# Inputs, ranks and slots of the first experts earlier, down biases in the last sums, row tiles at multiples of 128 bytes, in a two-block kernel with 32 routed experts

## The chip, the cores and the metric

One core of one Trainium2 chip runs the whole program. The metric is device time in microseconds (us). The engines are PE (TensorE; PEld its weight loads), DVE (VectorE), ACT (ScalarE), POOL (GpSimd) and SP (SyncE, which here only issues transfers).

## What is computed

Two blocks in sequence on 512 tokens of width 1024, all fp32. The first has a gated linear recurrence, retention and spatial gating, twice; the second is attention with a short convolution and then a mixture of experts. The change lies between the router of that mixture and the end:

```
h2 = modulate(x, g_norm2, sh2, sc2)               # 512 x 1024
logits = h2 @ w_router + b_router                 # 32 experts
top_logit, top_idx = top_k(logits, 4); gate = softmax(top_logit)
for each expert e, for the rows of h2 routed to it:
    gu = h2[rows] @ w_gate_up[e] + b_gate_up[e]   # 1024 x 2048
    y  = clamped_swiglu(gu) @ w_down[e] + b_down[e]
    moe[rows] += gate * y
x = x + gt2 * moe
out = rmsnorm(x, g_final)
```

Each expert brings 12 MB of fp32 weights, 384 MB for all.

## The kernel before

**Dense part and router, to about 1285 us.** Matmuls run as three passes: `split` (L288 to L291) makes a rounded high part on ACT (L289) and the remainder on DVE (L290), and PE multiplies high by high, high by low and low by high. `router` computes logits on the raw rows `hr`, takes the four best (`mask`), the position of each token within its expert (`pos`, by matmuls with triangular ones, `cum`), the counts (`cnt`), and the gates as high and low parts in `vals`. It also makes the modulated rows, in four pieces of 512 x 256 called `raw` and `tv`, scaled by 1/rms (`nat`), and stores them to DRAM as `h_rows`.

**Experts, from about 1295 us.** `moe` goes through `ORDER`: 0, 1, 16, 2, 17, 3 and so on. The 32 experts are ranked by load (`ranks`: matmuls `kc`, `rk`, `perm`); the upper 16 ranks are "wide" (up to 128 rows, three-pass weights through `wsplit`), the lower 16 "narrow" (64 rows, plain fp32 weights). Experts 0 and 1 are wide and are taken by their own number, before ranking. Weights come as 384 tiles of 1 MB: `wload` issues them on SP's queue into eight buffers in rotation. The fourth buffer first holds the staging of the gate-up bias, and the eighth lies on memory of `tv`.

For a pair of experts, `slots` finds which token sits in which row: it picks the pair's positions and gates by rank (`pick`), builds one-hot rows (`oh`), multiplies (`slot`, `slotT`), and makes indices; then POOL gathers their rows of `h_rows` into `xgn` (narrow) or `xg` (wide). `inputs` transposes them on PE (`xT<-xgn`, `xT<-xg`, L1518). Experts 0 and 1 need no DRAM: `first_slots` makes one-hots `hots` from `pos`, and `first_inputs` gathers by matmul (`xT<-hots,hr`, L1428), with evictions (`x<-xT`) by ACT (L1434) and DVE (L1432) in turn and a split. `gate_up`, `narrow_gate_up`, `down` and `narrow_down` compute; POOL adds the weighted results `ye` into the DRAM rows `x_rows` by index. `residual` (L1310) multiplies the down biases by the gates (`xt<-gb,gT`), adds them to `hr` and stores it as the first content of `x_rows`. At the end `finish` adds the last two experts from SBUF (`fx`) to the rows read back, and normalises.

**What sets the order.** In the router and the first expert the tile scheduler orders each engine, by priority (`high_priority(AHEAD)`) and by "not before" marks (`issue_after`, `behind`). From the second expert on `in_order` keeps the order in which the program is written. `work()` in `moe` is a list of steps; `fill` takes one step after each quarter of an expert's gate-up or down part, so that `slots` and `inputs` of later experts are spread over the current one. In the kernel before, the slots of 0 and 1 and then of 16 are made during expert 0 behind the second `first_inputs` and the ranks; those of 2 during expert 1:

```
slots[max(before(p - 3 - 2 * (narrow and p > 6)), 1 - narrow)].append((r, narrow))
```

Of the kernel before, what the change touches and what calls it, by code (L numbers as in the profile page):

```python
# [203 lines left out]
class Kern:  # L204
# [134 lines left out]
    def consts(self):  # L339
# [13 lines left out]
        self.mod = c.tile([128, 2, 48], F32, name="mod")  # L353

# [676 lines left out]
    def router(self):  # L1031
# [92 lines left out]
        nc.vector.tensor_add(pos, pos, pc[:, :128].rearrange("p (b e) -> p b e", b=4))  # L1124

# [5 lines left out]
        with tc.high_priority(AHEAD):  # L1131
            nc.vector.tensor_sub(G, lg, mx[:, :, 0:1].to_broadcast(B4))
            exp = nc.scalar.activation(G, G, AF.Exp).ins
            nc.vector.tensor_mul(G, G, mask)
            nc.vector.reduce_sum(gs, G, axis=X)
            nc.vector.reciprocal(gs, gs)
            nc.vector.tensor_mul(G, G, gs[:, :, None].to_broadcast(B4))
            nc.vector.tensor_copy(v[:, :, :, 2], G)
            gates = nc.vector.tensor_sub(v[:, :, :, 3], G, v[:, :, :, 2].bitcast(F32)).ins
# [102 lines left out]
    def wsplit(self, src):  # L1242
# [5 lines left out]
        with self.behind((self.hot,) if i == 0 else self.urgent if i < 8 else ()):  # L1248
            self.split(w, hi, lo)
# [60 lines left out]
    def residual(self):  # L1310
        nc, wk = self.nc, self.work
        st = wk.tile([128, D], F32, name="bst", tag="ye", bufs=2)
        gb = self.early.tile([128, D + 24], F32R, name="gb", bufs=1)
        gb = [gb[:, :T], gb[:, T:D]]
        gn = self.early.tile([128, T], F32, name="gn", tag="sg")[:, :384].rearrange("p (b m) -> p b m", b=4)
# [3 lines left out]
        nc.gpsimd.tensor_mul(st[:96], st[:96], self.g2[:96])  # L1319
        for h in range(2):  # L1320
            c = slice(h * 512, h * 512 + 512)
            nc.scalar.activation(gb[h][:96], st[:96, c], AF.Copy)
            nc.gpsimd.tensor_sub(gb[h][64:96], st[64:96, c], gb[h][64:96].bitcast(F32))
# [3 lines left out]
        gt = self.work2.tile([128, T], F32R, name="gT", tag="gT")  # L1327
        p = self.dn("gT")
# [15 lines left out]
    def ranks(self):  # L1344
# [36 lines left out]
        nc.vector.tensor_add(self.cnt, self.cnt, adj)  # L1381
        cm = wk.tile([128, 1], F32, name="cm")
# [5 lines left out]
        self.adj = adj  # L1388


    def narrow_consts(self):
        nc = self.nc
        v = self.vals.bitcast(F32)
        self.pg = self.xp.tile([128, 3, 4, 32], F32, name="pg")
        nc.vector.tensor_copy(self.pg[:, 0], self.pos)
        for c in range(2):
            nc.vector.tensor_copy(self.pg[:, 1 + c], v[:, :, :, 2 + c])
        nc.vector.tensor_add(self.pos, self.pos, self.adj[:, None, :].to_broadcast([128, 4, 32]))
        self.g2n = self.xp.tile([128, T], F32, name="g2n")
        for h in range(2):  # L1400
            nc.vector.tensor_copy(self.g2n[64 * h:64 * h + 64], self.g2[64 * h:64 * h + 64, h * 512:h * 512 + 512])
# [3 lines left out]
    def first_slots(self):  # L1405

        self.hots = self.xgp.tile([128, D], F32, name="hots", tag="xg").rearrange("p (q b s) -> p q b s", q=2, b=4)
        with self.tc.high_priority(AHEAD):
            for q in range(2):
                for b in range(4):  # L1410
                    hot = self.nc.vector.tensor_scalar(self.hots[:, q, b], self.rt[:, 292:420], self.pos[:, b, q:q + 1],
                                                       self.nat[:, b:b + 1], op0=OP.is_equal, op1=OP.mult).ins
                    if q == 0:
                        self.hot = hot

    def first_inputs(self, q):

        nc = self.nc
        xs = [], []
# [574 lines left out]
```

## Time and profile before

| | |
|---|---|
| median of 3 runs | 2409.7 us (2406.43 to 2410.49) |
| the profiled execution | 2409.16 us, of which the span of its trace is 2407.0 |
| mean granted TensorE clock | 0.986 of full speed |
| PE, DVE, ACT, POOL busy | 95%, 66%, 41%, 7% of the span |
| read from HBM | 550.7 MB |

An instruction is busy from its start to its end in the trace; idle time ahead of it is put down to the semaphore that came last. Times in the rows below count from the start of the span. Sixteen DMA engines serve the core; the DMA share is their mean busy share.

### The profile page before, as it was taken

Reading aid. Unit: us, or ns where it says so; the run is one execution under the profiler, and the core shown is the slowest. Engines: PE = TensorE matmul, PEld = TensorE weight load, DVE = VectorE, ACT = ScalarE, POOL = GpSimd, SP = SyncE. Lnnn points to the kernel's source line nnn. Section 1 sums busy time; section 2 is a strip of 40 time slices with the busy share of each in tenths; the row PEclk is TensorE's granted clock in tenths of the full one; section 3 lists DMA queues with packets and bytes.
Section 4 is the critical chain, followed back from the end, with each engine's and each line's share of the span. In section 5 each row is a group of like instructions: output and inputs, shape, how many; then the busy total and the mean of one; then the engine's idle time right before and its main releaser. Section 6 shows DMA issues by size and latency. Waiting matters only on the chain.

```text
span 2407.0 us, 29051 instructions
## 1 busy us (share of the span) xinstructions
PE 2286.2 (95%) x10863; PEld 1639.9 (68%) x10863; DVE 1589.7 (66%) x2487; ACT 982.7 (41%) x1166; POOL 163.1 (7%) x116
## 2 busy tenths in 40 slices
PE   8999999999999999999998789999999999999995
PEld 6778877777878878788876555555566555555552
DVE  8875764768747657786768856656666565656552
ACT  5632332435423324433455434334444443444421
POOL 0000000000000000000011111011111011011002
PEclk9999999999999999999998899999999999999998
DMA  4234334332342353422126689999999999999995
GB/s 163 86 112 122 99 117 129 125 118 86 94 151 88 99 164 109 142 74 83 55 88 236 251 337 401 407 395 403 395 401 392 403 397 400 403 396 404 412 399 227
DMA packets 109282, 563.59 MB, mean 234 GB/s; under 512 B 14440, under 2 KB 16872, under 8 KB 59984
## 3 DMA queue, kind: packets, MB, share of 16 engines
q1 hardware_dynamic: 95184, 532.33, 58.2%
q0 software_dynamic: 9200, 21.00, 3.2%
q10 hardware_dynamic: 4752, 8.36, 1.1%
q8 instruction: 87, 1.43, 0.2%
q14 instruction: 59, 0.48, 0.1%
HBM read 550.73 MB, written 18.87 MB: 237 GB/s over the span
## 4 chain that ended last, share of the span: by engine, by line
PE 81%; DMA 8%; DVE 7%; ACT 3%; issue 1%; POOL 0%; DVEq 0%; SPq 0%; ACTq 0%; POOLq 0%
PE prj L284 11%; PE prj L285 11%; PE prj L286 11%; PE pg L1549 7%; PE pd L1627 7%; PE pl L1550 7%; DMA w<-in_wgu 6%; PE pd L1650 4%; DVE wl L290 3%; PE pg L1588 2%; PE pl L1588 2%; ACT wh L289 2%; PE ada L796 1%; DMA w<-in_wdn 1%; PE cs L313 1%
## 5 line engine op out<-in xcount | busy, mean ns | idle before, releaser
L289 ACT ACTIVATE wh<-w 128x2048 fp32r<-128x2048 f32 (+3 forms) x382 | 560.4, 1469 | 587.2 <-PE prj L285 197.2
L290 DVE TENSOR_TENSOR wl<-w,wh 128x2048 fp32r<-128x2048 f32 (+3 forms) x382 | 660.2, 1734 | 205.3 <-ACT wh L289 204.8
L284 PE MATMUL prj<-ty,wh 128*128 128x512 f32 x880 | 353.0, 401 | 11.3 <-ACT wh L289 8.5
L285 PE MATMUL prj<-ty,wh 128*128 128x512 f32 x880 | 350.4, 398 | 1.2 <-DVE ty L823 0.9
L286 PE MATMUL prj<-ty,wl 128*128 128x512 f32 x880 | 349.7, 398 | 1.1 <-DVE wl L290 1.1
L1588 PE MATMUL pg<-w,xn 128*64 128x512 f32 x512 | 190.0, 600 | 39.4 <-DMA w<-in_wgu 39.3
L1549 PE MATMUL pg<-wh,x 128*128 128x512 f32 x512 | 210.1, 410 | 0.6 <-ACT wh L289 0.6
L1550 PE MATMUL pl<-wh,x 128*128 128x512 f32 x512 | 203.8, 398 | 0.0
L284 PEld LDWEIGHTS prj<-ty,wh 128*128 128x128 f32 x880 | 166.5, 189 | 50.4 <-ACT wh L289 10.6
L286 PEld LDWEIGHTS prj<-ty,wl 128*128 128x128 f32 x880 | 166.2, 189 | 41.1 <-DVE wl L290 2.4
L1569 DVE TENSOR_SCALAR li<-pl 128x512 f32<-128x512 f32 x48 | 33.0, 687 | 243.0 <-PE pl L1593 242.5
L285 PEld LDWEIGHTS prj<-ty,wh 128*128 128x128 f32 x880 | 166.4, 189 | 39.2 <-DVE ty L823 1.8
L1588 PE MATMUL pl<-w,xn 128*64 128x512 f32 x512 | 185.5, 595 | 0.0
L1568 ACT ACTIVATE sg<-pg 128x512 f32<-128x512 f32 x48 | 28.7, 597 | 308.6 <-PE pg L1593 260.8
L1588 PEld LDWEIGHTS pg<-w,xn 128*64 128x64 f32 x512 | 50.2, 136 | 125.2 <-DMA w<-in_wgu 69.7
L284 PE MATMUL prj<-tmix,wh 128*128 128x512 f32 x320 | 126.9, 398 | 0.3
L285 PE MATMUL prj<-tmix,wh 128*128 128x512 f32 x320 | 126.5, 395 | 0.0
L286 PE MATMUL prj<-tmix,wl 128*128 128x512 f32 x320 | 126.2, 395 | 0.0
L1650 PE MATMUL pd<-w,an 128*64 128x512 f32 x512 | 114.8, 596 | 7.6 <-DMA w<-in_wdn 6.1
L1549 PEld LDWEIGHTS pg<-wh,x 128*128 128x128 f32 x512 | 97.1, 190 | 32.5 <-issue 11.4
L1550 PEld LDWEIGHTS pl<-wh,x 128*128 128x128 f32 x512 | 97.3, 190 | 19.3
L1549 PE MATMUL pg<-wl,x 128*128 128x512 f32 x256 | 101.6, 397 | 0.4 <-DVE wl L290 0.4
(498 smaller groups left out, 3864.9 us busy)
## 6 DMA issues: line engine op xcount, KB each, us to landing
w<-in_wgu SPq DMA_DIRECT2D x256, 1024.0 KB, 12.6
w<-in_wdn SPq DMA_DIRECT2D x128, 1024.0 KB, 10.9
w<-in_w SPq DMA_DIRECT2D x118, 512.0 KB, 3.7
wa<-in_wada SPq DMA_DIRECT2D x48, 512.0 KB, 3.6
w<-in_wob SPq DMA_DIRECT2D x32, 384.0 KB, 3.1
w<-in_wg SPq DMA_DIRECT2D x16, 512.0 KB, 3.7
w<-in_wos SPq DMA_DIRECT2D x8, 512.0 KB, 3.6
w<-in_wo SPq DMA_DIRECT2D x8, 512.0 KB, 3.5
```

What stands on the lines that cost most here:

```text
L284: mm(ps, a[0], b[0], start=first, stop=False)
L285: mm(ps, a[0], b[1], start=False, stop=False)
L286: mm(ps, a[1], b[0], start=False, stop=last)
L289: ins = self.nc.scalar.activation(hi, src, AF.Copy).ins
L290: self.nc.vector.tensor_sub(lo, src, hi.bitcast(F32))
L1549: nc.tensor.matmul(pg, x[k], w[:, s, 0], start=first, stop=False)
L1550: nc.tensor.matmul(pl, x[k], w[:, s, 1], start=first, stop=False)
L1568: nc.scalar.activation(sg, pg, AF.Sigmoid, scale=1.702)
L1569: nc.vector.tensor_scalar(li, pl, 8.0, -6.0, op0=OP.min, op1=OP.max)
L1588: nc.tensor.matmul(p[64 * c:64 * c + 64], x[k], ws[c][:, s, h], start=k == 0, stop=False, skip_group_check=True)
L1627: nc.tensor.matmul(self.pd[n], a[:, k], w[:, s, n * 512:(n + 1) * 512], start=hf == 0 and k == 0 and a is ah and w is wh, stop=hf == 1 and ...
L1650: nc.tensor.matmul(pd[64 * n:64 * n + 64], a[:, k % 4, k // 4 * 64:k // 4 * 64 + 64], w[:, s, n * 512:(n + 1) * 512], start=k == 0, stop=k ...
```

## The change

It has eight parts.

1. Small pads move the tiles of rows and weights of the expert part to multiples of 128 bytes in SBUF. Weight buffers 0 to 3 were at 96 and buffer 7 at 224 bytes past a multiple of 256, buffers 4 to 6 at 128; now 0 to 3 and 7 are at 128 and 4 to 6 at 0.
2. `first_slots` and the first expert's `first_inputs` are stated in the router, behind `pos`, at twice the priority. The gates lose theirs. The second expert's one-hots follow behind the first eviction.
3. All scaling of `raw` and `tv` is done by ACT with POOL's adds (before, only the first piece), the last two pieces behind the second eviction.
4. `x_rows` gets `hr` without the bias, in one POOL transfer from the router. The bias products are prepared at the sixth expert (`biases`) and multiplied in the final sums (`bias_product`).
5. The first three weight splits stand behind the one-hots and the two evictions.
6. The low parts of the gate-up bias are made by POOL.
7. Ranks are stated before the first expert's loop; the slots of 16 and of 2 are made during expert 0, those of 0 and 1 during expert 1. `slots` picks with three multiplies, with no copied tile.
8. `pos` is completed at the last expert.

```diff
@@ -1122,21 +1124,25 @@
         pos = self.pos
         nc.vector.tensor_scalar(pos, mask, -4096.0, 4096.0, op0=OP.mult, op1=OP.add)
         nc.vector.tensor_add(pos, pos, pc[:, :128].rearrange("p (b e) -> p b e", b=4))
+        self.xs = {}
+        with tc.high_priority(2 * AHEAD):
+            self.first_slots()
+            for _ in self.first_inputs(0, self.prj, lambda: self.tl("mix", F32)):
+                pass
...
-        with tc.high_priority(AHEAD):
-            nc.vector.tensor_sub(G, lg, mx[:, :, 0:1].to_broadcast(B4))
...
+        nc.vector.tensor_sub(G, lg, mx[:, :, 0:1].to_broadcast(B4))
...
@@ -1146,14 +1152,16 @@
         for j in range(4):
             r = raw[j]
             row = shift[j // 2][:, j % 2 * 256:j % 2 * 256 + 256]
-            for b in range(0 if j else 4):
-                self.scaled = nc.scalar.activation(r[:, b], r[:, b], AF.Copy, scale=nat[:, b:b + 1]).ins
-                if b % 2:
-                    nc.gpsimd.tensor_add(r[:, b - 1:b + 1], r[:, b - 1:b + 1], row[:, None].to_broadcast([128, 2, 256]))
-            with tc.issue_after(exp), tc.issue_after(gates):
-                for b in range(4 if j else 0):
-                    nc.vector.scalar_tensor_tensor(r[:, b], r[:, b], nat[:, b:b + 1], row, op0=OP.mult, op1=OP.add)
+            with tc.high_priority(0 if j > 1 else AHEAD):
+                for b in range(4):
+                    with ExitStack() as c:
+                        if j > 1:
+                            c.enter_context(tc.issue_after(self.evicted[1]))
+                        nc.scalar.activation(r[:, b], r[:, b], AF.Copy, scale=nat[:, b:b + 1])
+                    if b % 2:
+                        nc.gpsimd.tensor_add(r[:, b - 1:b + 1], r[:, b - 1:b + 1], row[:, None].to_broadcast([128, 2, 256]))
             nc.sync.dma_start(self.h_d.rearrange("(b p) c -> p b c", p=128)[:, :, j * 256:j * 256 + 256], r)
+        nc.gpsimd.dma_start(self.x_d.rearrange("(b p) c -> p b c", p=128), self.hr)
         yield
     def rows_pools(self):
@@ -1245,7 +1253,7 @@
         lo = self.wls[i % 3].tile([128, 2048], F32R, name="wl", tag="wl", bufs=2 if i % 3 else 1)
-        with self.behind((self.hot,) if i == 0 else self.urgent if i < 8 else ()):
+        with self.behind(((self.hot, *self.evicted)[i],) if i < 3 else ()), self.tc.high_priority(AHEAD if i < 3 else 0):
             self.split(w, hi, lo)
         return hi, lo
...
-    def residual(self):
...
+    def down_bias(self, st, gb, gn, gt, g2, p):
...
-        for b in range(4):
-            rows = slice(b * 128, (b + 1) * 128)
-            for h in range(2):
-                p = self.dn("xt")
-                nc.tensor.matmul(p, gt[:96, rows], gb[h][:96], start=True, stop=True)
-                x = self.hr[:, b, h * 512:h * 512 + 512]
-                nc.vector.tensor_add(x, x, p)
-            nc.gpsimd.dma_start(self.x_d[rows], self.hr[:, b])
-        self.hrow.close()
-        self.xp = self.moe_pools.enter_context(self.tc.tile_pool(name="mx", bufs=1, reuse_waits="tile"))
+        return gt, gb
+    def bias_product(self, p, b, h, stop):
+        gt, gb = self.dbias
+        self.nc.tensor.matmul(p, gt[:96, b * 128:(b + 1) * 128], gb[:96, h * 512:h * 512 + 512], start=True, stop=stop)
+    def biases(self):
+        st = self.work.tile([128, D], F32, name="bst", tag="ye", bufs=2)
+        gb = self.early.tile([128, D + 24], F32R, name="gb", bufs=1)[:, :D]
+        gn = self.early.tile([128, T], F32, name="gn", tag="sg")[:, :384].rearrange("p (b m) -> p b m", b=4)
+        gt = self.work2.tile([128, T], F32R, name="gT", tag="gT")
+        self.dbias = self.down_bias(st, gb, gn, gt, self.g2, self.dn("gT"))
...
-    def narrow_consts(self):
-        nc = self.nc
-        v = self.vals.bitcast(F32)
-        self.pg = self.xp.tile([128, 3, 4, 32], F32, name="pg")
-        nc.vector.tensor_copy(self.pg[:, 0], self.pos)
-        for c in range(2):
-            nc.vector.tensor_copy(self.pg[:, 1 + c], v[:, :, :, 2 + c])
-        nc.vector.tensor_add(self.pos, self.pos, self.adj[:, None, :].to_broadcast([128, 4, 32]))
+    def narrow_gain(self):
         self.g2n = self.xp.tile([128, T], F32, name="g2n")
         for h in range(2):
-            nc.vector.tensor_copy(self.g2n[64 * h:64 * h + 64], self.g2[64 * h:64 * h + 64, h * 512:h * 512 + 512])
...
-        with self.tc.high_priority(AHEAD):
-            for q in range(2):
-                for b in range(4):
-                    hot = self.nc.vector.tensor_scalar(self.hots[:, q, b], self.rt[:, 292:420], self.pos[:, b, q:q + 1],
-                                                       self.nat[:, b:b + 1], op0=OP.is_equal, op1=OP.mult).ins
-                    if q == 0:
-                        self.hot = hot
-    def first_inputs(self, q):
+        self.evicted = []
+        for b in range(4):
+            self.hot = self.first_slot(0, b)
+    def first_slot(self, q, b):
+        return self.nc.vector.tensor_scalar(self.hots[:, q, b], self.rt[:, 292:420], self.pos[:, b, q:q + 1],
+                                            self.nat[:, b:b + 1], op0=OP.is_equal, op1=OP.mult).ins
+    def first_inputs(self, q, bank, buf):
...
+            self.evicted.append(self.split(t, *x))
...
-            nc.vector.tensor_mul(t, self.pg.rearrange("p c b e -> p (c b) e")[:, None].to_broadcast(S),
-                                 m[:, :, None, :].to_broadcast(S))
+            v = self.vals.bitcast(F32)
+            for j, x in enumerate((self.pos, v[:, :, :, 2], v[:, :, :, 3])):
+                nc.vector.tensor_mul(t[:, :, 4 * j:4 * j + 4], x[:, None].to_broadcast(S), m[:, :, None, :].to_broadcast(S))
...
                     self.fx[h, b] = self.gu("fx") if g == 0 else self.trp("fx") if h == 0 else self.dn("fx")
+                    self.bias_product(self.fx[h, b], b, h, False)
...
-        with self.tc.issue_after(self.hot):
-            for r in (32, 96):
-                nc.vector.scalar_tensor_tensor(self.bias[r:r + 32], st[r:r + 32], one[r:r + 32],
-                                               self.bias[r:r + 32].bitcast(F32), op0=OP.add, op1=OP.subtract)
+        for r in (32, 96):
+            lo = self.bias[r:r + 32]
+            nc.gpsimd.tensor_add(st[r:r + 32], st[r:r + 32], one[r:r + 32].to_broadcast([32, 1024]))
+            nc.gpsimd.tensor_sub(lo, st[r:r + 32], lo.bitcast(F32))
...
+            pad = lambda n: pool(f"mpad{n}").tile([128, n], F32, name=f"pad{n}")
+            pad(24)
             late = pool("mlate")
             self.work = late
+            pad(8)
             self.early = pool("mearly", 2)
...
-                    slots[max(before(p - 3 - 2 * (narrow and p > 6)), 1 - narrow)].append((r, narrow))
-            for _ in self.first_inputs(0):
-                pass
-            self.urgent = self.hot, self.scaled
+                    slots[before(p - 3 - 2 * (narrow and p > 6))].append((r, narrow))
             act = down = None
-            self.split_next(3)
+            self.split_next()
+            with self.behind(self.evicted[:1]):
+                for b in range(4):
+                    self.first_slot(1, b)
+                self.ranks()
+            self.split_next(2)
             ordered = c.enter_context(ExitStack())
             for p, (r, narrow) in enumerate(ORDER):
                 if p == 1:
                     ordered.enter_context(self.in_order())
                 def work():
                     if p == 0:
-                        yield
-                        yield from self.first_inputs(1)
-                        self.ranks()
-                        yield
-                        yield
+                        yield from self.first_inputs(1, self.dn, lambda: self.early.tile([128, T], F32, name="x0", tag="sg"))
+                        self.hrow.close()
+                        self.xp = c.enter_context(tc.tile_pool(name="mx", bufs=1, reuse_waits="tile"))
+                    if p == 1:
                         yield from self.slots(0, 0)
...
                     if t == 0 and hf == 0 and p == 0:
-                        with self.behind(self.urgent):
+                        with self.behind(self.evicted[:2]):
                             self.expert_consts()
-                    if t == 0 and hf == 1 and p == 0:
-                        with self.behind(self.urgent):
-                            self.residual()
-                            self.narrow_consts()
+                    if t == 0 and hf == 1 and p == 1:
+                        self.narrow_gain()
+                    if t == 0 and hf == 1 and p == 5:
+                        self.biases()
```

**POOL, from the router's raw rows to the first additions of results.** `x_rows<-hr` is the store of the rows, `tF` a row that is added, `xgn` and `xg` the gathered rows, `ye` the results. Before:

```order
L1152 TENSOR_TENSOR raw<-raw,tF 128x512 x2
L1319 TENSOR_TENSOR bst<-bst,g_11037 96x1024
L1323 TENSOR_TENSOR gb<-bst,gb 32x512 x2
L1339 DMA x_rows<-hr 128x1024 x4
L1501 MEMSET xgn 128x1024
L1502 DMA xgn<-h_rows,sn 128x1024
L1231 DMA x_rows<-ye,si 512x1024
L1501 MEMSET xg 128x1024
L1502 DMA xg<-h_rows,si 128x1024
L1501 MEMSET xg 128x1024
L1502 DMA xg<-h_rows,si 128x1024
L1231 DMA x_rows<-ye,si 512x1024
```

After:

```order
L1164 DMA x_rows<-hr 128x4x1024
L1162 TENSOR_TENSOR raw<-raw,tF 128x512 x4
L1754 TENSOR_TENSOR bst<-bst,one 32x1024 x2
L1755 TENSOR_TENSOR bias<-bst,bias 32x1024 x2
L1498 MEMSET xg 128x1024
L1162 TENSOR_TENSOR tv<-tv,tF 128x512 x4
L1498 MEMSET xgn 128x1024
L1498 MEMSET xg 128x1024
L1499 DMA xgn<-h_rows,sn 128x1024
L1499 DMA xg<-h_rows,si 128x1024 x2
L1239 DMA x_rows<-ye,si 512x1024 x2
L1239 DMA x_rows<-ye,sp 1024x512
```

The three gathers stand ahead of every `x_rows<-ye`; POOL has twelve additions and subtractions ahead of them, in place of five, and the bias of the down part (`gb`) is gone from here.

**DVE, from the counts to the first split of an expert's weights behind the inputs.** `hots` are the one-hots, `x` or `tmix` with `xT` the evictions of the gathered rows, `wl` the low part of a weight tile. Before:

```order
L1411 TENSOR_SCALAR hots<-rt,pos,nat_10797 128x128 x4
L1144 COPY cnt<-cnt 128x32
L1155 SCALAR_TENSOR_TENSOR raw<-raw,nat_10797,tF 128x256 x4
L1155 SCALAR_TENSOR_TENSOR tv<-tv,nat_10797,tF 128x256 x8
L1754 SCALAR_TENSOR_TENSOR bias<-bst,one,bias 32x1024
L1432 TENSOR_SCALAR x_10945<-xT,a_10479,mod 128x128
L1432 TENSOR_SCALAR x_10971<-xT,a_10479,mod 128x128
L1754 SCALAR_TENSOR_TENSOR bias<-bst,one,bias 32x1024
L290 TENSOR_TENSOR wl<-w,wh 128x2048 x2
L1432 TENSOR_SCALAR x_10945<-xT,a_10479,mod 128x128
L1432 TENSOR_SCALAR x_10971<-xT,a_10479,mod 128x128
L290 TENSOR_TENSOR wl<-w,wh 128x2048
```

After:

```order
L1150 COPY cnt<-cnt 128x32
L1410 TENSOR_SCALAR hots<-rt,pos,nat_10798 128x128 x4
L290 TENSOR_TENSOR wl<-w,wh 128x2048
L1428 TENSOR_SCALAR tmix<-xT,a_10480,mod 128x128
L1140 TENSOR_TENSOR tE<-tE 128x128
L1410 TENSOR_SCALAR hots<-rt,pos,nat_10798 128x128
L1141 TENSOR_REDUCE gs<-tE 128x4
L1410 TENSOR_SCALAR hots<-rt,pos,nat_10798 128x128
L1142 RECIPROCAL gs<-gs 128x4
L1410 TENSOR_SCALAR hots<-rt,pos,nat_10798 128x128
L1143 TENSOR_TENSOR tE<-tE,gs 128x128
L1428 TENSOR_SCALAR tmix<-xT,a_10480,mod 128x128
```

The first expert's four `hots` come straight behind the counts (before, behind the gates), and the scaling and the two bias parts are gone from between.

**SP, the loads of the first experts.** `w<-in_wgu` and `w<-in_wdn` are weight tiles, `h_rows<-raw` and `h_rows<-tv` the stores of the modulated rows. Before:

```order
L1239 DMA w<-in_wgu 128x2048 x5
L1156 DMA h_rows<-raw 128x4x256 x2
L1156 DMA h_rows<-tv 128x4x256 x2
L1239 DMA w<-in_wgu 128x2048 x2
L1318 DMA bst<-in_bdn 32x1024 x3
L1239 DMA w<-in_wdn 128x2048 x2
```

After:

```order
L1247 DMA w<-in_wgu 128x2048 x5
L1163 DMA h_rows<-raw 128x4x256 x2
L1247 DMA w<-in_wdn 128x2048
L1247 DMA w<-in_wgu 128x2048
L1247 DMA w<-in_wdn 128x2048
L1163 DMA h_rows<-tv 128x4x256 x2
L1247 DMA w<-in_wgu 128x2048 x5
```

Three tile loads now stand between the two pairs of stores, and all others behind the second pair.

## Rows read from the trace of the kernel before

**Rows 1.** Page, part 2: DMA share in 40 slices, in tenths

```profile
DMA  4234334332342353422126689999999999999995
```

**Rows 2.** Table of stretches: PE, PEld, DVE, ACT, POOL busy us; PEclk; DMA share; GB/s

```profile
1600.00:1800.00 200.00, 189.39 (x856) 115.31 (x854) 126.71 (x129) 83.81 (x68) 23.77 (x10) 1.00 1.00 402
1290.00:1404.00 114.00, 91.16 (x425) 72.27 (x426) 88.51 (x115) 55.37 (x52) 22.27 (x14) 0.90 0.74 277
```

**Rows 3.** Waits of PE, 1266 to 1480: releaser, total us, times, longest us

```profile
PE xT L1518 <- DMA xg<-h_rows,si: 6.7, 1, 6.7
PE xT L1518 <- DMA xgn<-h_rows,sn: 6.5, 1, 6.5
PE slot L1477 <- DVE oh L1466: 4.1, 1, 4.1
```

**Rows 4.** Timeline of PE: start, us, line, operation [idle before, releaser]

```profile
1280.53 2.72 PE L1428 MATMUL xT<-hots,hr 128*128 128x128 f32 x11 [3.25 <-DVE cnt L1144]
...
1294.30 0.87 PE L331 MATMUL rb<-ident,mod 128*128 128x128 f32 x6 [2.06 <-DVE x L1432]
...
1404.22 1.08 PE L1588 MATMUL pg<-w,xn 128*64 128x512 f32 x4
```

**Rows 5.** Timeline of POOL, 1266 to 1400

```profile
1273.83 2.58 POOL L1152 TENSOR_TENSOR raw<-raw,tF 128x512 f32<-128x512 f32 x2 [3.15 <-ACT raw L1150]
1298.69 2.39 POOL L1319 TENSOR_TENSOR bst<-bst,g 96x1024 f32<-96x1024 f32 x1 [22.29 <-DMA bst<-in_bdn]
...
1333.95 0.96 POOL L1501 MEMSET xgn<- 128x1024 f32 x1 [4.33 <-DMA x_rows<-hr]
1355.40 1.64 POOL L1502 DMA_INDIRECT xgn<-h_rows,sn  x1 [20.50 <-DVE sn L1222]
...
1387.23 2.52 POOL L1502 DMA_INDIRECT xg<-h_rows,si  x1 [1.66 <-issue]
```

**Rows 6.** Timeline of DVE in the router, 1274 to 1290

```profile
1274.98 0.29 DVE L1115 TENSOR_TENSOR tE<-tA,tB 128x128 fp32r<-128x128 f32 x1
1275.19 1.36 DVE L1132 TENSOR_TENSOR tE<-tB,mx 128x128 f32<-128x128 f32 x1
...
1281.98 3.25 DVE L1155 SCALAR_TENSOR_TENSOR tv<-tv,nat,tF 128x256 f32<-128x256 f32 x8
...
1288.11 1.28 DVE L1754 SCALAR_TENSOR_TENSOR bias<-bst,one,bias 32x1024 fp32r<-32x1024 f32 x1
```

**Rows 7.** Groups of DVE by line, 1290 to 1404: busy us, mean ns | idle before

```profile
L290 DVE TENSOR_TENSOR wl<-w,wh 128x2048 fp32r<-128x2048 f32 x24 | 55.4, 2321 | 14.5 <-ACT wh L289 14.4
L1338 DVE TENSOR_TENSOR hr<-hr,xt 128x512 f32<-128x512 f32 x8 | 5.5, 684 | 0.6 <-PE xt L1336 0.6
```

**Rows 8.** Groups of PE by line, 1300 to 1345

```profile
L1336 PE MATMUL xt<-gb,gT 96*128 96x512 f32 x8 | 3.1, 403 | 0.0
```

**Rows 9.** Table of stretches again, four short ones (columns as in rows 2)

```profile
1340.00:1350.00 10.00, 6.70 (x22) 4.97 (x22) 9.97 (x16) 3.83 (x2) 0.00 (x0) 0.83 0.82 312
1360.00:1370.00 10.00, 9.50 (x37) 7.82 (x38) 2.50 (x2) 3.51 (x5) 0.00 (x0) 0.75 0.28 99
1390.00:1400.00 10.00, 3.26 (x13) 2.47 (x12) 5.80 (x5) 2.98 (x3) 3.83 (x2) 0.79 0.99 383
1400.00:1412.00 12.00, 12.00 (x54) 5.93 (x54) 3.76 (x4) 2.88 (x3) 0.00 (x0) 0.89 0.48 168
```

**Rows 10.** Timeline of SP's queue behind the router: issues

```profile
1283.67 1.95 SPq L1156 DMA_DIRECT2D h_rows<-tv  x2
1289.42 0.82 SPq L1239 DMA_DIRECT2D w<-in_wgu  x2
```

**Rows 11.** Table of stretches, two tiles into buffers 2, 3, then 4, 5

```profile
1680.10:1685.08 4.98, 4.98 (x22) 1.74 (x19) 0.39 (x1) 0.60 (x1) 0.00 (x0) 1.00 1.01 423
1685.08:1690.05 4.97, 4.97 (x22) 3.98 (x22) 2.14 (x4) 1.92 (x1) 0.00 (x0) 1.00 1.01 420
```

**Rows 12.** Timeline of PE in the final sums

```profile
2381.62 0.50 PE L1690 MATMUL fx<-ys,to 64*128 64x512 f32 x1 [0.38 <-ACT ys L289]
```

More of the change, by code (lines that the diff above doesn't have):

```diff
@@ L353, in consts @@
         self.mod = c.tile([128, 2, 48], F32, name="mod")
+        c.tile([128, 8], F32, name="pad")
     def lru_scale(self):
@@ L1307, in behind @@
             yield
[L1310 to L1315 removed]
+    def down_bias(self, st, gb, gn, gt, g2, p):
+        nc = self.nc
         for r in range(0, 96, 32):
             nc.sync.dma_start(st[r:r + 32], self.d["bdn"])
[L1319 removed]
+        nc.gpsimd.tensor_mul(st[:96], st[:96], g2[:96])
         for h in range(2):
             c = slice(h * 512, h * 512 + 512)
[L1322 to L1323 removed]
+            nc.scalar.activation(gb[:96, c], st[:96, c], AF.Copy)
+            nc.gpsimd.tensor_sub(gb[64:96, c], st[64:96, c], gb[64:96, c].bitcast(F32))
         v = self.vals.bitcast(F32)
@@ L1420, in first_inputs @@
         for hf in range(2):
-            with self.tc.high_priority(0 if q else AHEAD):
-                p = self.trp("xT")
-                t = self.early.tile([128, 4, 128], F32, name="x0", tag="sg")
-                for k in range(4):
-                    c = 4 * hf + k
-                    pk = p[:, k * 128:(k + 1) * 128]
-                    for b in range(4):
-                        nc.tensor.matmul(pk, self.hr[:, b, c * 128:(c + 1) * 128], self.hots[:, q, b],
-                                         start=b == 0, stop=b == 3)
-                    g, o = self.a2[:, c:c + 1], self.mod[:, 0, 24 + c:25 + c]
-                    if k % 2:
-                        nc.vector.tensor_scalar(t[:, k], pk, g, o, op0=OP.mult, op1=OP.add)
-                    else:
-                        nc.scalar.activation(t[:, k], pk, AF.Identity, scale=g, bias=o)
-                x = [self.hpool.tile([128, 4, 128], F32R, name="x", tag="h", bufs=8) for _ in range(2)]
-                self.split(t, *x)
-                for i in range(2):
-                    xs[i].extend(x[i][:, k] for k in range(4))
+            p = bank("xT")
+            t = buf().rearrange("p (k s) -> p k s", k=4)
+            for k in range(4):
+                c = 4 * hf + k
+                pk = p[:, k * 128:(k + 1) * 128]
+                for b in range(4):
+                    nc.tensor.matmul(pk, self.hr[:, b, c * 128:(c + 1) * 128], self.hots[:, q, b],
+                                     start=b == 0, stop=b == 3)
+                g, o = self.a2[:, c:c + 1], self.mod[:, 0, 24 + c:25 + c]
+                if k % 2:
+                    nc.vector.tensor_scalar(t[:, k], pk, g, o, op0=OP.mult, op1=OP.add)
+                else:
+                    nc.scalar.activation(t[:, k], pk, AF.Identity, scale=g, bias=o)
+            x = [self.hpool.tile([128, 4, 128], F32R, name="x", tag="h", bufs=8) for _ in range(2)]
+            self.evicted.append(self.split(t, *x))
+            for i in range(2):
+                xs[i].extend(x[i][:, k] for k in range(4))
             yield
@@ L1668, in last_rows @@
         self.ys, self.fx = [], {}
+        nc.vector.tensor_add(self.pos, self.pos, self.adj[:, None, :].to_broadcast([128, 4, 32]))
         self.xr = [[self.hpool.tile([128, T], F32, name="xr", tag="h") for _ in range(4)] for _ in range(2)]
@@ L1770, in moe @@
             self.nw, self.ns, self.xp = 0, 0, None
-            self.first_slots()
             self.expert_bias(first)
-            self.xs, self.acts, self.idx, self.gate, self.put, self.xg, self.at, self.expert = ({} for _ in range(8))
+            self.acts, self.idx, self.gate, self.put, self.xg, self.at, self.expert = ({} for _ in range(7))
             self.wides, self.ready = self.wide_tiles(), {}
@@ L1950, in final @@
             nc.sync.dma_start(gf, bass.AP(tensor=d["gfin"].tensor, offset=d["gfin"].offset, ap=[[0, 128], [1, D]]))
+            st, gb, g2 = (wk.tile([128, D], F32R if n == "fgb" else F32, name=n, bufs=1) for n in ("fst", "fgb", "fg2"))
+            gn, gt = (wk.tile([128, T], F32R if n == "fgt" else F32, name=n, bufs=1) for n in ("fgn", "fgt"))
+            self.gate_rows(g2)
+            self.dbias = self.down_bias(st, gb, gn[:, :384].rearrange("p (b m) -> p b m", b=4), gt, g2, self.dn("gT"))
             for b in range(4):
@@ L1953, in final @@
                 nc.sync.dma_start(x, self.x_d[b * 128:(b + 1) * 128])
+                for h in range(2):
+                    p = self.dn("fb")
+                    self.bias_product(p, b, h, True)
+                    nc.vector.tensor_add(x[:, h * 512:h * 512 + 512], x[:, h * 512:h * 512 + 512], p)
                 sq = wk.tile([128, D], F32, name="fsq")
```

24 lines of the change are left out of this document (12 added, 12 removed).

## The prediction

> **What bounds the kernel now.** I read from coarse to fine. The page's picture of the span in 40 slices comes first: a slice is 60.2 us, and the DMA digits are 1 to 5 through the dense part, then 2, 6, 6, 8, and 9 from the slice that begins near 1444 us to the last but one [rows 1]. The table of stretches sharpens that: 1600 to 1800 us runs at a DMA share of 1.00 and 402 GB/s [rows 2]. So from there to the last weight tile the experts are bound by transfers, and PE, though busy 189 of 200 us, has slack. Nothing in that stretch becomes shorter by moving work of an engine; it can only **begin earlier**. The place to look is what lies ahead, from the router at 1270 us to the narrow third expert (number 16), whose first matmul starts at 1404.22 [rows 4]. Its tiles free the weight buffers for which the next loads wait; behind it the DMA queue no longer runs dry. Between 1290 and 1404 us the DMA share is 0.74 at 277 GB/s, PE is busy 91.2 us of 114 and DVE 88.5 [rows 2]. No engine is full there: it is a chain with holes.
>
> The list of PE's waits names the holes: 6.7 us for the gathered rows of expert 2, 6.5 us for those of expert 16, 4.1 us for the one-hot rows `oh` behind the slots [rows 3]. POOL shows why the gathers are late: it issues the first at 1355.40, after 20.5 us of waiting for the indices `sn`, and the first of the other two at 1387.23 [rows 5]. PE needed them at once. Ahead of that, PE waits 3.25 us before the first expert's gather by matmul and 2.06 us behind it [rows 4]. After each hole the granted clock is low for a while: 0.83, 0.75, 0.79 and 0.89 in four windows [rows 9], which is a mixture of the 1.2 and 2.4 GHz levels.
>
> **The change, part by part,** as shifts of the moment at which expert 16 starts (1404.2 us), negative for earlier.
>
> 1. First expert's inputs in the router. Its one-hots now stand directly behind positions and counts, and the gate chain, the scaling of the rows (3.25 us of DVE for eight of its twelve operations) and the two bias parts (1.28 each) no longer stand ahead of the evictions [rows 6]. The four one-hots can be there 1.5 to 2.5 us sooner than 1280.53, and the 2.06 us behind DVE mostly go; the whole could give 5.5 us. Against it: POOL's adds now run longer just there. One row prices that: a subtraction of 128x128 took 1.36 us on DVE where its neighbour of the same size took 0.29, and POOL's two adds (1273.83 to 1276.41) lay across it [rows 5, 6]. POOL now has two further raw adds (1.3 us each), four bias operations (about 2.4 each, from the 96x1024 one) and four later adds [rows 5], some 17 us, and every DVE operation on two SBUF tiles that meets one may lose a us. I take **-3** (-5.5 to +2). The Trainium skill, SBUF — State Buffer, section "SBUF: two separate sides", says the same port pair is locked for a whole instruction and the loser blocks entirely; by that rule each of the first split and the two low parts of the inputs could wait out a whole bias operation; this term would be +2 and the time 2393.5.
> 2. The residual bias leaves the first expert. Its eight 96-row matmuls (3.1 us busy with overlap, 0.40 us each; at the pitch of its neighbours 1.9) leave PE [rows 8], and eight additions of 0.68 us, 5.5 in all, leave DVE [rows 7]. They come back at the sixth expert, which is DMA-bound. **-2** (-3.1 to -1.9).
> 3. Gathers earlier. Ranks and the slots of experts 16 and 2 are computed while expert 0 runs, so POOL issues all three gathers before the first `x_rows<-ye`, some 30 us ahead of use. The waits of 6.5 and 6.7 go: **-13.2** (-13.2 to -9).
> 4. The 4.1 us for `oh`: DVE was behind after the residual. The slots of experts 0 and 1 now stand at that place with the same one-hot, but 5.5 us less is queued before it. **-3** (-4.1 to +4).
> 5. Clock. A window's share at the lower level is (1 - clock)/0.5: 3.4, 5.0, 4.2 and 2.6 us in the four windows, of which PE was busy about 3.4, 4.5, 2.2 and 2.6; half of that, 6.3 us, was lost [rows 9]. Without the holes most returns: **-5** (-6.3 to -2).
> 6. New waits. DVE is nearly as loaded as PE in a wide expert (24 low parts of weights alone are 55.4 us [rows 7]), and the ranks and one pick of three multiplies now stand between the first of them. SP is the other place: the stores `h_rows<-tv`, at 1283.67 before [rows 10], now wait for ACT's scaling behind the inputs' split and for POOL's adds, to about 1300, and every load behind them waits too. The eighth tile, whose buffer lies on the second half of those rows, can start only when they have landed, about 1305 (before, the loads followed at 1289.42, 5.7 us behind the stores' issue [rows 10]); PE wants it after seven others, which at 24 tiles in a stretch of some 94 us is 27 us behind its start near 1291, at 1318; with landing and splitting ahead of that I put the last harmless moment for the stores' issue at 1305. **+5** (0 to +12).
> 7. The end. Eight bias matmuls join the final sums. Four stand where PE waited 0.38 us for `ys` [rows 12], four while DVE still works on the first half. 4 x 0.40 - 0.38 is 1.2 at most: **+0.6** (0 to 1.2).
> 8. Tiles at multiples of 128 bytes. Before, weight buffers 0 to 3 and 7 start off such multiples and 4 to 6 on them. Two tiles into buffers 2 and 3 take 4.98 us at 423 GB/s, the next two into 4 and 5 take 4.97 at 420 [rows 11]. **0** (-6 to 0; the lower end is below).
>
> The storing of `x_rows` in one piece from the router, the picks by three multiplies, `narrow_gain` and the moved `pos` cost nothing I can see: they lie beside POOL or DVE idle time behind them, each under 1 us if that cover is gone, which term 6 holds.
>
> Sum: -3 - 2 - 13.2 - 3 - 5 + 5 + 0.6 = **-20.6 us**. A check from the other side: the stretch of 114 us needs at least 91.2 - 6.3 - 1.9 = 83 us of PE, 88.5 - 5.5 = 83 of DVE, and 0.74 x 114 = 84 of DMA, of which 5 are the 2.1 MB of `x_rows` (512 rows of 4 KB, at 402 GB/s) that leave it: 79. I leave it at 94. As the transfers behind are at their limit, the shift carries through to the end one for one. The profiled execution took 2409.16 us, 0.5 below the median of 2409.7: 2409.2 - 20.6 = **2388.5 us**.
>
> **The rivals.**
> - *DVE takes the place of the gathers.* It is the engine that lost least. If the wait for `oh` stays (term 4 at 0 and not -3) and new waits are 12 and not 5, the gain is 10 smaller: 2398.5. For it: DVE is busy 88.5 of 114 us; against: it loses 5.5 us just there. 0.17.
> - *The alignment counts.* The two readings of 423 and 420 GB/s differ by 0.7% [rows 11]. If that were the size of a misplaced start and it went for all, the 352 tiles of the DMA-bound stretch (384 less the first 32), at 2.49 us each, would give 876 x 0.7% = 6 us: 2382.5; with term 6 at 0 too, 2377. The Trainium skill, DMA: Bandwidth & Descriptors, section "How a descriptor splits into AXI transactions", says a transaction must start at a multiple of 256 bytes, so that a piece that starts elsewhere pays for the bytes before it; that would help the tiles that move onto such a multiple, and the trace's buffers, none on one, cannot show it. Between two misplaced kinds the trace shows no order, so I give it 0.10.
> - *The SP queue is held: slower.* Place: the stores `h_rows<-tv`, ahead of all loads from the tenth tile on. If their adds run last, behind a memset that waits for the first inputs to be read, the loads stand still meanwhile. Each us behind 1305 is then lost one for one, and from 1326 on the gain of 20.6 is gone. With the memset where it is now (1333.95 [rows 5]) and four adds of 1.3 behind it, the stores go at 1339, 34 us too late: 2388.5 + 34 = 2422.5. For it: the queue is in order; against: ACT's scaling follows work that ends near 1291. 0.07.
> - *No change.* The holes are refilled to within 4 us by a mixture of the first and third: 2408. 0.06.
>
> **How the numbers follow.** My forecast has the rest, 0.60. Faster by over 0.2% (about 4.8 us, what a measurement of this kernel can tell from no change) is the forecast, the first two rivals: 0.87. Same 0.06, slower 0.07. The range begins with terms 1, 2, 4 and 5 at their good ends (6 us together), the 6 us of alignment and half of term 6 gone: 2388.5 - 14.5 = 2374. It ends with the first rival and term 4 at its bad end, 2398.5 + 4 = 2403 rounded up. Outside lie the slower rival, no change and a few in 100 of the rest, a little under 2 in 10.
>
> **What would show it.** Right: expert 16's first narrow matmul near 1384; no wait of PE for `xgn` or `xg`; both gathers issued by 1340; the clock at 1.00 from the first expert on; DMA share 0.9 from 1390. Wrong: a PE wait for `wl` or a weight tile near 1315 to 1325 (term 6), `oh` still over 4 us (term 4), two tiles in less than 4.9 us (term 8), or a late second stretch whose start moves but whose end does not.

## The result, and the profile after

The changed kernel takes **2387.8 us** (median of 4 runs, 2386.22 to 2389.87) against 2409.39 for the kernel before, run beside it: a ratio of 0.9913 [0.9896, 0.993], 21.6 us faster. The profiled execution took 2387.84 us, its span 2386.1 (2407.0 before).

The page's picture of the span, against [rows 1]: the DMA engines are full (9 tenths) one slice earlier.

```profile
DMA  4233334333242353422125899999999999999995
```

Waits of PE between 1260 and 1480 us, columns as in [rows 3]. Those for `xgn` and `xg` and the 4.1 us for `oh` are gone: the 2.2 us for `oh` in this list are another wait, at 1434.97, behind the start of expert 16. At the top stand 7.5 us for `hots`; before, PE waited 3.25 us at that place [rows 4].

```profile
PE xT L1424 <- DVE hots L1410: 7.5, 4, 4.5
...
PE pg L1546 <- DVE wl L290: 2.5, 2, 1.8
PE slot L1474 <- DVE oh L1468: 2.2, 1, 2.2
```

POOL's timeline, against [rows 5]: the two gathers are issued 25 and 41 us sooner; but the bias parts (L1754, L1755) now stand between 1267.69 and 1276.4 us.

```profile
1267.69 3.92 POOL L1754 TENSOR_TENSOR bst<-bst,one 32x1024 f32<-32x1024 f32 x2
1271.69 4.75 POOL L1755 TENSOR_TENSOR bias<-bst,bias 32x1024 fp32r<-32x1024 f32 x2
...
1330.58 1.20 POOL L1499 DMA_INDIRECT xgn<-h_rows,sn  x1 [14.81 <-issue]
1346.39 1.03 POOL L1499 DMA_INDIRECT xg<-h_rows,si  x1 [14.60 <-DVE si L1222]
```

DVE in the same microseconds: the four one-hots take 7.56 us.

```profile
1269.96 7.56 DVE L1410 TENSOR_SCALAR hots<-rt,pos,nat 128x128 f32<-128x128 f32 x4
```

The start of expert 16 on PE, at 1404.22 in [rows 4]:

```profile
1373.80 1.08 PE L1585 MATMUL pg<-w,xn 128*64 128x512 f32 x4
```

The table of stretches, columns as in [rows 2] and [rows 9]: first the time from the first gate-up matmul to expert 16, before and after (PE's clock 0.89 and 0.98), then the changed kernel alone: a clock of 1.00 from 1310 us, the transfers full from 1400 on, and the DMA-bound stretch unchanged (402 GB/s before).

```profile
1294.96:1404.22 109.26, 88.67 (x406) 69.83 (x404) 83.55 (x111) 54.47 (x49) 22.27 (x14) 0.89 0.73 274
1287.31:1373.80 86.49, 81.25 (x401) 65.00 (x400) 82.77 (x107) 59.29 (x57) 17.57 (x10) 0.98 0.81 296
...
1310.00:1374.00 64.00, 61.99 (x303) 49.50 (x303) 62.72 (x72) 43.02 (x36) 9.53 (x6) 1.00 0.90 331
1400.00:1470.00 70.00, 66.68 (x298) 41.42 (x297) 49.63 (x64) 29.40 (x24) 9.54 (x5) 0.98 0.98 391
1600.00:1800.00 200.00, 191.93 (x856) 116.55 (x856) 128.64 (x135) 84.17 (x68) 23.79 (x10) 0.98 1.00 401
```

So the gain is not all where it was forecast. The traces of seven kernels at seven places (us from the start of the span; weight tiles counted from 0, each at the end of its last packet; e1 to e11 are the experiments below):

| kernel | router's logits transposed | first gate-up matmul | expert 16 | tile 40 | tile 96 | last tile | end |
|---|---|---|---|---|---|---|---|
| before | 1272.2 | 1295.0 | 1404.2 | 1432.9 | 1591.0 | 2377.7 | 2407.0 |
| **after** | 1261.1 | 1287.3 | 1373.8 | 1403.2 | 1567.0 | 2355.7 | 2386.1 |
| e1_pad32 | 1261.3 | 1283.9 | 1392.8 | 1420.8 | 1579.6 | 2367.8 | 2397.2 |
| e2_nopad | 1270.6 | 1297.4 | 1384.7 | 1414.0 | 1576.9 | 2365.5 | 2398.1 |
| e5_bias_dve | 1259.8 | 1279.5 | 1365.1 | 1394.5 | 1559.8 | 2346.7 | 2377.1 |
| e7_slots_back | 1264.5 | 1290.5 | 1395.3 | 1422.9 | 1586.9 | 2373.6 | 2406.0 |
| e11_four | 1259.1 | 1276.2 | 1363.0 | 1392.2 | 1551.9 | 2339.3 | 2368.1 |

From before to after, stretch by stretch: dense part -11.1, router to the first gate-up +3.4 (22.8 to 26.2), wide experts -22.7 (109.2 to 86.5), expert 16 to tile 40 +0.7, to tile 96 +5.7 (158.1 to 163.8), the DMA-bound rest +2.0, the end +1.1: -20.9. For the first of these the forecast had 0.

### The profile page after: what moved, and what is told of

Its sections match the earlier page's. It is cut to its first block, busy times and chain, and to the rows that moved or that the text cites. A ratio compares the mean times of both kernels' runs of the same rounds, so it can differ in the third digit from the quotient of the medians.

```text
span 2386.1 us, 29072 instructions
## 1 busy us (share of the span) xinstructions
PE 2278.2 (95%) x10863; PEld 1643.4 (69%) x10863; DVE 1599.5 (67%) x2492; ACT 987.8 (41%) x1178; POOL 176.0 (7%) x123
## 4 chain that ended last, share of the span: by engine, by line
PE 80%; DVE 8%; DMA 7%; ACT 3%; issue 1%; DVEq 0%; ACTq 0%; POOLq 0%
PE prj L284 11%; PE prj L285 10%; PE prj L286 10%; PE pg L1546 7%; PE pd L1624 7%; PE pl L1547 7%; DMA w<-in_wgu 6%; PE pd L1647 4%; DVE wl L290 3%; PE pg L1585 2%; PE pl L1585 2%; ACT wh L289 2%; PE ada L798 1%; PE cs L313 1%; DMA w<-in_wdn 1%
## 5 line engine op out<-in xcount | busy, mean ns | idle before, releaser
L284 PE MATMUL prj<-ty,wh 128*128 128x512 f32 x880 | 348.3, 396 | 11.9 <-ACT wh L289 8.3
L285 PE MATMUL prj<-ty,wh 128*128 128x512 f32 x880 | 345.6, 393 | 1.6 <-DVE ty L825 1.2
L1546 PEld LDWEIGHTS pg<-wh,x 128*128 128x128 f32 x512 | 96.9, 189 | 31.1 <-issue 11.4
```

What stands on the lines that cost most here:

```text
L284: mm(ps, a[0], b[0], start=first, stop=False)
L285: mm(ps, a[0], b[1], start=False, stop=False)
L1546: nc.tensor.matmul(pg, x[k], w[:, s, 0], start=first, stop=False)
```

## The experiments

Theory at the start: slots and gathers give the wide experts' part, and the dense part's 11 us come from where a matmul operand starts. Rival: they come from the transfers or from the moved router.

**The pad alone, and all but the pad.** Part 1 of the change speaks of the expert part, and the diff printed there leaves out one of its pads: a tile of 32 bytes in the pool of constants. It moves the dense part's row tiles `ty` and `tl` from 96 bytes past a multiple of 128 onto one, and in the expert part the rows and weight buffers 0 to 3; `wh`, `wl` and `tmix` stay on multiples of 128 (addresses of the built kernels).

```diff
 e1_pad32 (before, plus)          e2_nopad (after, less)
+        c.tile([128, 8], F32, name="pad")
-        c.tile([128, 8], F32, name="pad")
```

> The kernel before with one thing of the change: the pad of 32 bytes among the constants, which moves the dense part's tiles ty from 96 to 0 bytes past a multiple of 128 (tmix stays at 0). Theory A (the start of ty in SBUF sets the time of a matmul that reads it): the matmuls prj<-ty go from a median of 395 to 389 ns, prj<-tmix stay, the first expert tile loads leave 11 us earlier, and the whole is 2398 us, 11 below the kernel before. Theory B (the dense part was quicker through the new order or by chance of the execution): prj<-ty stay at 395 ns and the whole at 2409.

> The changed kernel without that pad of 32 bytes; the pads of the expert part stay. Theory A: prj<-ty back at 395 ns and the whole 11 us slower than the changed kernel, 2399. Theory B: no difference, 2388.

Measured: e1 2398.72 us, ratio 0.9951 [0.9934, 0.9968]; e2 2399.07, 0.9951 [0.9934, 0.9967]. The pad is worth 10.6 us on the old kernel and 11.3 on the new. Where it acts shows in the matmuls of the dense part: the view of one line's instructions by tile gives the duration in ns, least/median/most (the numbers at a line's end count the forms of a sample). First the kernel before:

```profile
L284 PE MATMUL prj<-ty,wh x880: 388/396/796, 6.9 to 1166.0; 128*128 128x512 f32 x176
L284 PE MATMUL prj<-tmix,wh x320: 387/389/504, 161.0 to 1265.6; 128*128 128x512 f32 x160
```

Then e1:

```profile
L284 PE MATMUL prj<-ty,wh x880: 387/389/796, 6.9 to 1154.9; 128*128 128x512 f32 x176
```

The same matmul took 396 ns with `ty` as the moving operand and 389 with `tmix`; with the pad both take 389. There are 2640 of the first kind in three lines, and PE is busy 1038.7 us with them instead of 1053.1. Not every shape gains: `vp<-wh,ty`, where `ty` is the stationary operand and `wh` moves 256 columns, goes from a median of 280 to 283 ns. The dense part as a whole is 10.9 us shorter. The transfers have no part in it, as PE waits 0.2 us for them before 1172 us in the kernel before. The rival falls. In the expert part the pad brings nothing: from the router's transposes to the end it is 1135.9 us in e1 and 1134.8 before.

**Which step.** Two other pads in the kernel before, a single run each.

```diff
+        c.tile([128, 16], F32, name="pad")      (e3_pad64)
+        c.tile([128, 24], F32, name="pad")      (e4_pad96)
```

> The kernel before with a pad of 64 bytes: ty starts 32 bytes past a multiple of 128. Theory A with a step of 64 or 128 bytes: prj<-ty at 395 ns, whole 2409. Theory A with a step of 32 bytes would have shown no difference before. Theory B: 395 ns too.

> The kernel before with a pad of 96 bytes: ty starts 64 bytes past a multiple of 128. Theory A with a step of 64 bytes: prj<-ty at 389 ns, whole 2398; with a step of 128 bytes: 395 ns, 2409. Theory B: 395 ns.

Measured: e3 (32 past) 2407.79 us, median 396 ns; e4 (64 past) 2399.61 us, 392 ns. Starts at 0 and 64 past are fast, at 32 and 96 slow: the step is 64 bytes, with a rest for 128 (the router's transposes come at 1263.1 us in e4, 1261.3 in e1, 1271.9 in e3, 1272.2 before). As `wh` stood still in all four, these runs don't tell the start of `ty` from its distance to the other operand's.

**The bias parts off POOL.** In the changed kernel, the two low parts by one DVE operation each, stated behind the one-hots.

```diff
-        for r in (32, 96):
-            lo = self.bias[r:r + 32]
-            nc.gpsimd.tensor_add(st[r:r + 32], st[r:r + 32], one[r:r + 32].to_broadcast([32, 1024]))
-            nc.gpsimd.tensor_sub(lo, st[r:r + 32], lo.bitcast(F32))
+        with self.tc.issue_after(self.hot):
+            for r in (32, 96):
+                nc.vector.scalar_tensor_tensor(self.bias[r:r + 32], st[r:r + 32], one[r:r + 32],
+                                               self.bias[r:r + 32].bitcast(F32), op0=OP.add, op1=OP.subtract)
```

> The changed kernel with the low parts of the gate-up bias made by DVE again, behind the first expert's one-hots, and no longer by POOL. Theory C (POOL's bias operations hold up DVE's one-hots): the four hots take 1.3 us and not 7.6, PE's waits for them (7.3 us) go to under 2, the first gate-up matmul starts 4 to 5 us earlier than 1287.3, expert 16 at 1369 to 1370, and the whole is 4 us faster, 2384. Theory D (the first inputs' start is hidden by something behind them): the one-hots are quick, the whole stays at 2388.

Measured: 2380.0 us, 0.9881 [0.9864, 0.9897], 7.8 below the changed kernel. The one-hots in DVE's timeline of e5:

```profile
1268.42 1.12 DVE L1410 TENSOR_SCALAR hots<-rt,pos,nat 128x128 f32<-128x128 f32 x4
```

The four one-hots take 1.12 us instead of 7.56. From the router's transposes to the first gate-up it is 19.7 us, 3.1 less than before: what term 1 forecast, and what the POOL operations had hidden. The whole gains twice the 4 us that I expected.

**The bias of the sixth expert.** It comes back at a place where the queue of loads is in order. SP's queue of the changed kernel: no issue from 1472.10 to 1483.00, since the bias's load waits for a buffer, and every weight load behind it with it.

```profile
1472.10 0.33 SPq L1247 DMA_DIRECT2D w<-in_wgu  x1
1483.00 1.27 SPq L1322 DMA_DIRECT2D bst<-in_bdn  x3
```

The view of SP's waits names the buffer, that of the results `ye`:

```profile
SPq L1322 <- DMA x_rows<-ye,si: 10.5, 1, 10.5
```

Then PE waits 5.6 us for the gates `gn`, and the granted clock is 0.65 in the stretch that holds this wait; the wait, and the two stretches (columns as in [rows 2]):

```profile
PE gT L1332 <- DVE gn L1330: 5.6, 1, 5.6
...
1481.00:1488.00 7.00, 6.64 (x30) 3.18 (x26) 5.13 (x6) 0.79 (x1) 1.44 (x2) 1.00 0.74 225
1488.00:1494.00 6.00, 0.73 (x4) 0.70 (x5) 4.06 (x4) 2.27 (x3) 2.51 (x2) 0.65 1.02 386
```

e6 states the bias five weight tiles later; e9 states it four later, with the transposes of the gates apart from it, in the eighth expert.

```diff
 e6_bias_later
-        self.dbias = self.down_bias(st, gb, gn, gt, self.g2, self.dn("gT"))
+        self.dbias = self.down_bias(st, gb, gn, gt, self.g2, self.trp("gT"))
...
-                    if t == 0 and hf == 1 and p == 5:
+                    if t == 1 and hf == 2 and p == 5:
 e9_gates_split
...
-                    if t == 0 and hf == 1 and p == 5:
+                    if t == 0 and hf == 2 and p == 5:
                         self.biases()
+                    if t == 0 and hf == 0 and p == 7:
+                        self.gate_columns(self.gn, self.dbias[0], self.trp("gT"))
```

> The changed kernel with the down biases prepared five weight tiles later in the sixth expert. Theory E (their three loads stand in SP's queue before weight tiles and wait there for the buffer of ye, which starves the DMA engines from 1483 on): the load issues have no hole of 11 us, tile 72 lands 4 us earlier relative to tile 40 (93 us behind it and not 97), and the whole is 3 to 5 us faster, 2384. Theory F (the DMA-bound stretch takes up the hole, or the 97 us have another cause): tile 72 stays 97 us behind tile 40, the whole at 2388.

> The changed kernel with the preparation of the down biases cut in two: loads, POOL, ACT and the copies gn four weight tiles later in the sixth expert, PE's transposes gT at the start of the eighth. Theory E2 (what costs is PE's wait of 5.6 us for gn with the low clock behind it, since PE and DMA are nearly level in this stretch): no wait for gn, tile 96 lands 4 to 6 us earlier relative to tile 40 (158 to 160 us behind it and not 163.6; 158.2 in the kernel before), the whole 4 us faster, 2384. Theory F (the DMA-bound stretch takes it up, as it did with the later loads alone): tile 96 stays 163 to 164 us behind tile 40, the whole at 2388.

Measured: e6 2387.81 us, 0.9904 [0.9887, 0.992]; e9 2386.6, 0.9907 [0.989, 0.9923]. In e6 the hole in the loads is gone (tile 72 lands 93.9 us behind tile 40, 96.9 in the changed kernel), but PE still waits 7.1 us for `gn`, and by tile 96 all is given back (164.0 us behind tile 40, 163.8 in the changed kernel). In e9 that wait is gone too and tile 96 lands 160.7 behind tile 40; the total doesn't change beyond its uncertainty. So hole and wait together cost some 3 us at tile 96; that these reach the end isn't shown.

**The order of the slots.** The changed kernel, with the slots in the order of the kernel before: 0 and 1, then 16 during expert 0, those of 2 during expert 1.

```diff
-                    slots[before(p - 3 - 2 * (narrow and p > 6))].append((r, narrow))
+                    slots[max(before(p - 3 - 2 * (narrow and p > 6)), 1 - narrow)].append((r, narrow))
...
-                    if p == 1:
                         yield from self.slots(0, 0)
```

> The changed kernel with the slots in the order of the kernel before: 0 and 1, then 16 during expert 0, those of 2 during expert 1. Theory G (the earlier gathers are the main gain): PE waits for xg again, 6 to 8 us with the clock's fall, expert 16 starts 8 to 10 us later than 1373.8, the whole is 6 to 9 us slower, 2395. Rival: the rest of the change already lets the gathers come in time, or the transfers behind take it up; the whole stays within 2 us of 2388.

Measured: 2405.13 us, 0.9981 [0.9971, 0.9991] (10 runs): 17 us of the 21.6 are gone, over twice what I expected. The wide experts take 104.8 us instead of 86.5. Both waits come back; PE's waits of e7:

```profile
PE xT L1515 <- DMA xgn<-h_rows,sn: 8.5, 1, 8.5
PE xT L1515 <- DMA xg<-h_rows,si: 7.8, 1, 7.8
```

**The end.** The first four bias products stated ahead, in the last narrow expert; a single run.

```diff
+            if t == 2 and (r, 1) == ORDER[-1]:
+                for h in range(2):
+                    for b in range(2):
+                        self.open_part(h, b)
...
```

> The changed kernel with the four bias products of the first half of the final sums stated two tiles ahead of the end of the last expert's down part, where PE waits for weights. If they cost what they look like, DVE's first addition xr<-xr,fx comes 7.4 us behind the last tile's landing, as in the kernel before, and not 9.1: 1.7 us less. If the sums wait for ys anyway, no difference.

Measured: 2384.93 us. The first addition to `xr` starts 5.2 us behind the last tile, 6.9 in the changed kernel, 5.2 before. In the time of a single run 2.9 us can't be told from nothing; the place shows 1.7.

**The weight buffers.** The changed kernel without its two pads ahead of the buffers, so that these start 128 or 224 bytes past a multiple of 256.

```diff
-            pad(24)
             late = pool("mlate")
             self.work = late
-            pad(8)
```

> The changed kernel without the two pads of the expert part (the pad among the constants stays): weight buffers 4 to 6 go from 0 to 128 bytes past a multiple of 256, buffer 7 from 128 to 224, and the results ye from 0 to 96. Theory H (the start of a transfer's tile does not matter here, and the gain of alignment is all PE's): 2388, no difference, and eight weight tiles still take 19.7 to 20 us between 1550 and 1700. Rival (a start on a multiple of 256 bytes, or of 64 for the rows, makes transfers quicker): 2392 to 2394.

Measured: 2392.09 us, 0.9939 [0.9922, 0.9955], 4 us slower, though the two intervals overlap. But its rate between 1600 and 1800 us is that of the changed kernel (399 and 401 GB/s):

```profile
1600.00:1800.00 200.00, 187.84 (x856) 117.40 (x856) 128.15 (x135) 84.01 (x69) 23.78 (x10) 1.00 1.00 399
```

From tile 96 to the last it takes 792.2 us, where the kernel before, with its buffers misplaced, took 786.7 and the changed one 788.7. So most of the loss lies there in this trace; whose it is stays open. The Trainium skill, DMA: Bandwidth & Descriptors, section "How a descriptor splits into AXI transactions", has a cost for pieces that start off a multiple of 256 bytes; these runs neither show it nor rule it out.

For PE the pads ahead of the buffers aren't all gain. In the wide experts' gate-up matmul both operands, `wl` and `x`, start on multiples of 128 in both kernels (addresses of the built kernels), and the two pads move `wl` by 128 bytes. First the changed kernel, then e12:

```profile
L1546 PE MATMUL pg<-wl,x x256: 387/395/497, 1288.3 to 2289.4; 128*128 128x512 f32 x128
L1546 PE MATMUL pg<-wl,x x256: 387/389/628, 1287.7 to 2291.9; 128*128 128x512 f32 x128
```

So two operands on multiples of 128 don't make 389 ns sure. What sets the 395 stays open; `pd<-wh,ah` goes the other way, 395 ns with the pads and 400 without.

**Put together.** e10 is e5, e8 and e9 in one; e11 is e10 with half of the router's raw additions on DVE, behind the one-hots.

```diff
-                        nc.gpsimd.tensor_add(r[:, b - 1:b + 1], ...)
+                        with tc.issue_after(self.hot):
+                            (nc.gpsimd if j > 1 else nc.vector).tensor_add(r[:, b - 1:b + 1], ...)
```

> The changed kernel with three edits together: bias low parts by DVE, the preparation of the down biases in two, the four bias products two tiles earlier. If their effects add up: 2380 less 1.7 and less 4, 2374; if the cut brings nothing, 2378.

> The three edits and a fourth: the four additions for the first half of the rows go from POOL to DVE, behind the first one-hots. If POOL's additions are what lengthens DVE's small operations (1.3 us each and not 0.3) ahead of the one-hots, PE's waits for tE and for hots fall from 6.5 us to about 3 and the whole is 3 us below the three edits, 2371; if DVE's 2.7 us for them delay the evictions as much, no difference.

Measured: e10 2375.88 us, 0.9865 [0.9849, 0.9882]; e11 **2373.92**, 0.9855 [0.9839, 0.9872]: 13.9 below the changed kernel and 35.6 below the one before. Of e10 and e11 the intervals overlap; that the last step helps isn't shown.

## Why the prediction was right, and where not

The time was forecast at 2388.5 us and came at 2387.8. That the sum was right is luck: two errors of some 10 us cancel. It carried a shift of 20.6 us to the end undiminished, where about half arrives, and it gave the alignment 0, where it gives 10.6. e2, all of the change but the pad, shows the first: expert 16 starts 19.5 us sooner (20.6 forecast), tile 96 lands 14.1 sooner, the last 12.2, the end comes 8.9 sooner.

- **Term 1** (first inputs, -3): wrong as built, +3.4. That the rest of the step gives its 3 us, e5 shows; the POOL operations, bounded by a row in which one subtraction lost a us, cost 6.5 here. Four one-hots, each with one full-size SBUF operand (`rt`, beside two columns of scalars), lost 1.6 us each in the mean ((7.56 - 1.12) / 4). The Trainium skill, SBUF — State Buffer, section "SBUF: two separate sides", says that the port pair that the two engines share goes to one of them for a whole instruction; the trace agrees: the four end at 1271.70, 1274.11, 1276.52 and 1277.53, each 0.08 us behind the end of a POOL instruction, three of the bias parts and then the memset of `xg`. The upper bound of +2 was worked out with too few victims.
- **Terms 2 to 6** (-18.2 together): -22.7. The gathers are issued by 1346 (1340 forecast) and nobody waits for them; the three waits of 6.7, 6.5 and 4.1 us are gone whole, 17.3 us, where terms 3 and 4 had 16.2. PE is busy 7.4 us less from the first gate-up matmul to expert 16 (88.7 and 81.3), at a clock of 0.98 for 0.89, where terms 2 and 5 had 7. Term 6's +5 was too dark, and that is most of the difference: SP's stores went at 1299.49, 5.5 us ahead of the harmless limit, and PE's other waits in this stretch come to 5.2 us, 3.2 before. e7 says that 18.3 us of this stretch hang on the order of the slots alone, as much as terms 3 and 5 together (18.2).
- **Term 2's second half**, "they come back at the sixth expert, which is DMA-bound": failed. There a load that waits for its buffer holds all weight loads behind it for 11 us, and PE waits 5.6 us for the gates. The step from tile 40 to tile 96 is 5.7 us longer, and e9, without either, wins 3.1 of it back; the other 2.6 stay open.
- **The carry, "one for one"**: failed for that reason first, and by about 2 us in the DMA-bound rest, a difference that the profiles don't tell from chance: over all of them it lies between 785 and 792 us. In e2 a further 3.3 us are lost behind the last tile.
- **Term 7** (the end, +0.6, at most 1.2): +1.1 in the trace. e8 puts 1.7 on the bias products.
- **Term 8** (alignment, 0): failed by the largest size. I asked the transfers alone; the rows of PE, 396 ns by `ty` beside 389 by `tmix`, stood in the trace of before. The sign for expert 16, "near 1384", was missed by 10 us for it (1373.8; 1384.7 in e2).

Of the rivals, the first came true in part, for `hots` and not for `oh`. The second was right that alignment counts and wrong in the mechanism: the 10.6 us come through PE's operand and not through the transfers, whose share, if they have one, is not shown. The third, SP's stores held up, didn't happen.

## What to carry to other kernels

Compare the median durations of one matmul over its different operands: where a shape costs 2% more with one tile than with another, ask where the tiles start, and try a pad by itself. Before an operation goes to POOL, look at which DVE operations will run beside it, not at POOL's idle time; the short ones pay. And a shift ahead of a DMA-bound stretch is not carried whole if the change puts new waits into that stretch, here a load that must wait for its buffer in the in-order queue of loads, and gates that PE must wait for.

## What I had not expected of the hardware

In the dense part, a 128x512 matmul has a median of 396 ns when its moving operand `ty` starts 32 or 96 bytes past a multiple of 128, 392 at 64 past and 389 at 0; what the start of the other operand does to it, no run here isolates. Three POOL operations of 32x1024 in a row and a memset stretched four DVE operations of 128x128 from 1.12 us to 7.56, though these have a single full-size SBUF operand each.
